# Forty-four unread one-pass products behind the low-rank gate product of layer one

## The chip, the cores and the metric

The kernel runs on one core of a Trainium2 chip. The metric is the device time of one execution in microseconds, as the median of several runs. A core has a matrix engine (TensorE; PE in the profile, and PEld for its loading of stationary operands), a vector engine (VectorE, DVE), an activation engine (ScalarE, ACT), a general engine (GpSimd, POOL) and a queue for transfers (SyncE, SP). Each works through its own list of instructions in order, and semaphores tie the lists together.

## The reference

The reference is two layers of an encoder trunk on 256 tokens and 16 learned meta tokens, D = 2048. Cut to what matters here:

```
def _layer(h, w_in, gla_w_up, gla_b_up, ...):
    proj = jnp.einsum('bld,dp->blp', h, w_in)
    gq, gk, gv, gr, glr, nq, nk, nv = jnp.split(proj, points, axis=-1)
    y_gla = _gla_mixer(gq, gk, gv, gr, glr, gla_w_up, gla_b_up, gla_norm_w)
    y_na = _na_mixer(nq, nk, nv, na_rel_bias)
    mix = jnp.einsum('blm,md->bld', jnp.concatenate([y_gla, y_na], axis=-1), w_out)
    h = _layer_norm(DEEPNORM_ALPHA * h + mix, ln1_w, ln1_b)
    ff = ... square(relu(h @ w_ff1)) @ w_ff2
    return _layer_norm(DEEPNORM_ALPHA * h + ff, ln2_w, ln2_b)

def _gla_mixer(q, k, v, r, gate_lr, w_up, b_up, norm_w):
    lr = gate_lr.reshape(B, L, 2, GLA_RANK)
    g = jax.nn.log_sigmoid(jnp.einsum('blzr,zrk->blzk', lr, w_up) + b_up) / GLA_TAU
    ...
```

The part of interest is `glr`: 32 columns of the input projection (rank 16, forward and backward), from which the decay gates of the linear attention are made. Everything is float32.

## The kernel before

**Precision.** A float32 operand is split into a high part of type fp32r and a low remainder of the same type. A product of two operands is then three one-pass products, high by high, high by low and low by high, accumulated in one PSUM bank. Weights come from memory in tiles of 128 x 1024 float32 (`raw`); ScalarE casts the high part (`wh`, line 217) and VectorE subtracts it to get the low part (`wl`, line 218). There are three buffers of each, and a tile is made while others are used. A tile holds eight blocks of 128 x 128 and feeds 24 products. The activations `x` lie in 16 pairs of high and low, 128 rows by 272 columns each (L = 272 tokens with the meta tokens).

**Narrow work.** Products with fewer than 256 columns (the intra-chunk scores, the neighbourhood attention, per-token sums) take plain float32 operands, with no split. Transposes go through TensorE against an identity matrix.

**The order.** The program is written out in one order. `by_k` computes four or eight outputs at once, over the 16 blocks of the contraction (line 303); `by_m` computes one output after another (`eight`, line 252; `sixteen`, lines 259 to 267). Between the pieces `pump` takes steps of two queues of generators, foreground and background, so that small work is strewn between the big products. In layer one `by_k` computes keys and the first half of the values, then `by_m` the second half of the values and the queries, while the foreground queue holds the generator `gates`.

**The gates.** `gates` has these steps: load the small weights; split the low-rank weights `wlr` into `ws`, 64 columns with 32 high and 32 low; then the low-rank product, 32 instructions at line 468, two for each of 16 blocks of x, into columns 0 to 271 of a bank `ps` of the four background banks. The output has 64 rows, high weights in the first 32 and low weights in the next. Then ScalarE copies rows 32 to 63 (`lrt`, line 473), VectorE adds the two halves (474), and `stack` makes `lr`, a high copy, a low copy and another high copy under one another (344, 345). In the next steps two products for each head (line 486) take `lr` and the up-projection, and ScalarE and VectorE make the gates from the result (487 to 492). In the same stretch `v_rows` transposes finished values (line 516).

The bank has 512 columns. Columns 272 to 511 of `ps` are not used.

Of the kernel before, what the change touches and what calls it, by code (L numbers as in the profile page):

```python
# [14 lines left out]
P = 128  # L15
D = 2048
DC = D // P
T = 256
NM = 16
L = T + NM  # L20
# [38 lines left out]
class Trunk:  # L59
# [392 lines left out]
    def gates(self):  # L452
        nc, e, l = self.nc, self.ep, self.l
        if l == 0:
            self.load_gates()
            self.consts()
        yield
        ws = e.tile([P, DC, 64], F32R, name="ws", tag="ws")
        self.split(self.wlr.rearrange("p (k c) -> p k c", c=32), ws[:, :, :32], ws[:, :, 32:])
        yield True  # L460
        uh = e.tile([LRK, 2, GH * GDK], F32R, name="uph", tag="uph")
        up = e.tile([LRK, 2, GH * GDK], F32R, name="up", tag="up")
        ps = self.bank()
        o = ps[:, :L]
        for k in range(DC):
            xh, xl = self.x[k]
            for m, r in ((64, xh), (32, xl))[::-1 if k == DC - 1 else 1]:
                nc.tensor.matmul(o[:m], lhsT=ws[:, k, :m], rhs=r[:, :L], start=k == 0 and m == 64,  # L468
                                 stop=k == DC - 1 and m == 64)
        t = e.tile([32, L], F32, name="lrt", tag="lrt")  # L470
        lr = e.tile([LRK, L], F32R, name="lr", tag="lr")
        nc.gpsimd.memset(lr[96:LRK, :].bitcast(F32), 1.0)
        nc.scalar.copy(t, o[32:64])
        nc.vector.tensor_tensor(t, o[:32], t, ALU.add)
        self.stack(t, lr, 32, (0, 64), 32)
        for d, w in enumerate(self.wup):
            w = w[:LRK]
            nc.scalar.copy(uh[:, d], w)
            nc.vector.tensor_scalar(w, w, self.sel[:, 0:1], None, ALU.mult)
            nc.vector.scalar_tensor_tensor(up[:, d], uh[:, d].bitcast(F32), self.sel[:, 1:2], w, ALU.mult, ALU.add)  # L480
        yield True
        for h in range(GH):
            z = [self.bank()[:, :L] for _ in range(2)]
            g = e.tile([P, 2, L], F32, name="gt", tag="gt", bufs=2)
            for d in range(2):
                nc.tensor.matmul(z[d], lhsT=up[:, d, h * GDK:h * GDK + GDK], rhs=lr, start=True, stop=True)
                nc.scalar.activation(g[:, d], z[d], AF.Abs)
            nc.scalar.activation(g, g, AF.Exp, scale=-1.0)
            nc.scalar.activation(g, g, AF.Ln, bias=self.one)
            for d in range(2):  # L490
                nc.vector.scalar_tensor_tensor(g[:, d], z[d], 0.0, g[:, d], ALU.min, ALU.subtract)
            nc.scalar.activation(self.decay[h], g, AF.Exp, scale=1 / TAU)
            yield h < GH - 1

    def ev_q(self, m, ps):
        self.nc.scalar.mul(self.qk[m][:, 1, :self.n], ps, GDK ** -0.5)
# [757 lines left out]
```

## Time and profile before

| | before |
|---|---|
| median of 3 runs | 2328.91 us |
| lowest and highest | 2328.5 and 2329.83 us |
| the profiled execution | 2329.64 us |
| span of its instructions | 2327.8 us |
| mean granted TensorE clock | 0.999 |
| busy: PE, PEld, DVE, ACT, POOL | 2318.9, 2202.1, 1522.8, 1222.8, 129.4 us |
| instructions on PE | 18052 |
| bytes moved | 419.01 MB |

The profile is one execution, with times from the start of its first instruction. A line such as "L252 PE MATMUL mm<-x,wh 128*128 128x272 f32" names the line of the kernel, the engine, the operation, the tiles written and read, the weights in rows by columns, and the moving operand in partitions by columns. Both plain float32 and fp32r stand as f32 in PE's rows; a plain float32 product has two records, a one-pass product has one. "Busy" is the time in which at least one instruction of the engine is in flight, and PE's instructions overlap, so the length of one is more than the step from one to the next.

### The profile page before, as it was taken

What the parts mean: (1) busy time and instruction counts of PE and PEld (TensorE: products, weight loads), DVE (VectorE), ACT (ScalarE), POOL (GpSimd) and SP (SyncE); (2) the same over time, 40 slices, a digit from 0 to 9 for tenths busy, and PEclk for the clock granted to TensorE, in tenths of its full rate; (3) what the DMA queues carried; (4) which work ended last, traced back from release to release, by engine and by line L of the source; (5) the groups of instructions that cost most, each with busy time, mean ns of one, the idle gap of its engine ahead of it and who ended that gap; (6) DMA issues with size and microseconds to landing.
All of it is one profiled execution on the core that took longest, in us unless ns stands there. A gap on an engine that the chain in (4) does not pass through costs nothing.

```text
span 2327.8 us, 44399 instructions
## 1 busy us (share of the span) xinstructions
PE 2318.9 (100%) x18052; PEld 2202.1 (95%) x18052; DVE 1522.8 (65%) x2440; ACT 1222.8 (53%) x2104; POOL 129.4 (6%) x200
## 2 busy tenths in 40 slices
PE   9999999999999999999999999999999999999998
PEld 9999999999999999999999899989988888888888
DVE  5588777775544455547576787778866545666655
ACT  5666665564433344444456666655655334555443
POOL 0021110110000000000020111100100000000000
PEclk9999999999999999999999999999999999999999
DMA  8554545555555566655555555555666565656664
GB/s 265 155 163 155 151 146 169 173 181 181 181 178 179 179 180 182 181 179 176 181 187 165 173 168 156 158 166 186 192 198 191 190 198 190 192 198 213 199 194 150
DMA packets 118300, 419.01 MB, mean 180 GB/s; under 512 B 13512, under 2 KB 14024, under 8 KB 118096
## 3 DMA queue, kind: packets, MB, share of 16 engines
q1 hardware_dynamic: 117808, 415.65, 57.2%
q8 instruction: 141, 2.31, 0.4%
q14 instruction: 63, 0.52, 0.1%
q10 hardware_dynamic: 288, 0.52, 0.1%
HBM read 414.03 MB, written 2.10 MB: 179 GB/s over the span
## 4 chain that ended last, share of the span: by engine, by line
PE 97%; DVE 1%; issue 1%; ACT 0%; DMA 0%; POOL 0%; DVEq 0%; ACTq 0%; SPq 0%; POOLq 0%
PE mm L252 56%; PE mm L264 30%; PE mm L303 4%; PE mm L313 2%; PE bg L303 1%; PE bg L827 1%; PE mm L766 1%; DVE wl L218 0%; PE bg L627 0%; PE bg L468 0%; DVE acc L1057 0%; PE mm L792 0%; PE bg L955 0%; PE mm L516 0%; PE bg L678 0%
## 5 line engine op out<-in xcount | busy, mean ns | idle before, releaser
L218 DVE TENSOR_TENSOR wl<-raw,wh 128x1024 fp32r<-128x1024 f32 (+1 forms) x770 | 938.3, 1225 | 645.1 <-ACT wh L217 546.0
L217 ACT CAST wh<-raw 128x1024 fp32r<-128x1024 f32 (+1 forms) x770 | 805.5, 1047 | 790.5 <-PE mm L252 383.8
L252 PE MATMUL mm<-x,wh 128*128 128x272 f32 (+3 forms) x4544 | 805.7, 294 | 0.0
L252 PEld LDWEIGHTS mm<-x,wh 128*128 128x128 f32 x4544 | 646.8, 188 | 14.9 <-PE mm L766 0.6
L252 PE MATMUL mm<-x,wl 128*128 128x272 f32 (+3 forms) x2432 | 519.7, 284 | 0.0
L252 PEld LDWEIGHTS mm<-x,wl 128*128 128x128 f32 x2432 | 390.8, 188 | 0.0
L252 PE MATMUL mm<-y,wh 128*128 128x272 f32 (+1 forms) x1440 | 235.0, 285 | 0.0
L252 PEld LDWEIGHTS mm<-y,wh 128*128 128x128 f32 x1440 | 199.7, 188 | 0.1
L264 PE MATMUL mm<-x,wh 128*128 128x512 f32 x832 | 193.8, 390 | 0.0
L264 PEld LDWEIGHTS mm<-x,wh 128*128 128x128 f32 x832 | 154.3, 188 | 31.0
L252 PE MATMUL mm<-u,wh 128*128 128x272 f32 (+1 forms) x1056 | 172.1, 285 | 0.0
L264 PE MATMUL mm<-y,wh 128*128 128x512 f32 x688 | 162.3, 389 | 0.0
L264 PEld LDWEIGHTS mm<-y,wh 128*128 128x128 f32 x688 | 128.6, 188 | 26.8 <-issue 0.4
L252 PE MATMUL mm<-y,wl 128*128 128x272 f32 (+1 forms) x720 | 146.5, 285 | 0.0
L252 PEld LDWEIGHTS mm<-u,wh 128*128 128x128 f32 x1056 | 146.3, 188 | 0.0
L264 PE MATMUL mm<-u,wh 128*128 128x512 f32 x496 | 118.3, 391 | 0.0
L252 PEld LDWEIGHTS mm<-y,wl 128*128 128x128 f32 x720 | 112.6, 188 | 0.0
L264 PEld LDWEIGHTS mm<-u,wh 128*128 128x128 f32 x496 | 90.9, 188 | 17.7
L252 PE MATMUL mm<-u,wl 128*128 128x272 f32 (+1 forms) x528 | 107.3, 284 | 0.0
L264 PEld LDWEIGHTS mm<-x,wl 128*128 128x128 f32 x832 | 98.4, 188 | 2.0
L264 PE MATMUL mm<-x,wl 128*128 128x256 f32 x832 | 98.8, 276 | 0.0
L264 PEld LDWEIGHTS mm<-y,wl 128*128 128x128 f32 x688 | 84.3, 188 | 3.0 <-DVE wl L218 0.2
(286 smaller groups left out, 2297.4 us busy)
## 6 DMA issues: line engine op xcount, KB each, us to landing
raw<-in_wff SPq DMA_DIRECT2D x512, 512.0 KB, 3.6
raw<-in_win SPq DMA_DIRECT2D x190, 512.0 KB, 4.0
raw<-in_wout SPq DMA_DIRECT2D x64, 512.0 KB, 3.6
nb<-in_nab SPq DMA_DIRECT2D x16, 352.0 KB, 4.3
xraw<-in_xT SPq DMA_DIRECT2D x7, 272.0 KB, 4.5
out<-out SPq DMA_DIRECT2D x5, 256.0 KB, 3.1
brow<-in_norm SPq DMA_DIRECT2D x4, 256.0 KB, 5.1
gw<-in_wup SPq DMA_DIRECT2D x4, 196.0 KB
```

What stands on the lines that cost most here:

```text
L217: self.nc.scalar.copy(h, r)
L218: self.wl = self.nc.vector.tensor_tensor(lo, r, h.bitcast(F32), ALU.subtract).ins
L252: mm(o, lhsT=self.block(w, j), rhs=rhs, start=first and not i, stop=last and i == len(TURNS[once]) - 1)
L264: self.nc.tensor.matmul(o, lhsT=self.block(both[j // 8][low], j % 8), rhs=rhs, start=first and not i + j, stop=bool(last and i and j == 15 ...
L303: self.nc.tensor.matmul(ps[g + m][:, :n], lhsT=self.block(parts[p][0], 4 * j + m if first else 2 * m + j), rhs=acts[k + j][parts[p][1]][:, ...
L313: self.nc.tensor.matmul(o, lhsT=self.block(both[low], i), rhs=rhs, start=not low and k + i % 2 == 0, stop=k == DC - 2 and i % 2 == 1 and n ...
L766: nc.tensor.matmul(ps[hh][:, t * NKEY:t * NKEY + NKEY], lhsT=q[hs, NM + t * P:NM + t * P + P], rhs=k[hs, t, :], start=True, stop=True)
L827: nc.tensor.matmul(po[t][hs, :P], lhsT=v2[ts, hs] if rest else v1[:, t, hs], rhs=p2[ts, hh, :] if rest else p1[:, 2 * hh + t, :], start=re ...
```

## The change

After the 32 instructions of the low-rank product of layer one, and before the copy that reads its result, 44 more products are issued. Number i takes as weights the first 128 columns of x block i modulo 16 and as moving operand the first n columns of the next block, the high parts for even i and the low parts for odd i. Each starts afresh and writes columns 272 to 271 + n of the same bank `ps`. Nothing reads these columns. The widths n are 128 twelve times, 136 twelve times, 240 and 128 in turn six times, and 64 eight times. The operands are of type fp32r. In layer two nothing is added.

```
@@ -467,6 +467,8 @@
             for m, r in ((64, xh), (32, xl))[::-1 if k == DC - 1 else 1]:
                 nc.tensor.matmul(o[:m], lhsT=ws[:, k, :m], rhs=r[:, :L], start=k == 0 and m == 64,
                                  stop=k == DC - 1 and m == 64)
+        if not l:
+            self.narrow(ps)
         t = e.tile([32, L], F32, name="lrt", tag="lrt")
         lr = e.tile([LRK, L], F32R, name="lr", tag="lr")
@@ -491,6 +493,13 @@
+
+    def narrow(self, ps):
+
+        sizes = [P] * 12 + [P + 8] * 12 + [240, P] * 6 + [64] * 8
+        for i, n in enumerate(sizes):
+            w, v = (self.x[(i + d) % DC][i % 2] for d in (0, 1))
+            self.nc.tensor.matmul(ps[:, L:L + n], lhsT=w[:, :P], rhs=v[:, :n], start=True, stop=True)
```

## The prediction

> **What bounds the kernel now.** I read the page first, then the busy time by stretches, the timeline around the place of the change, the chain of waits, and last the rows that can price a product the kernel does not contain yet.
>
> From the page: busy time by engine, two rows of the 40 slices, and the shares of the chain that ended last.
>
> ```profile
> span 2327.8 us, 44399 instructions
> ...
> PE 2318.9 (100%) x18052; PEld 2202.1 (95%) x18052; DVE 1522.8 (65%) x2440; ACT 1222.8 (53%) x2104; POOL 129.4 (6%) x200
> ...
> PE   9999999999999999999999999999999999999998
> ...
> PEclk9999999999999999999999999999999999999999
> ...
> PE 97%; DVE 1%; issue 1%; ACT 0%; DMA 0%; POOL 0%; DVEq 0%; ACTq 0%; SPq 0%; POOLq 0%
> ```
>
> TensorE is busy in 2318.9 of 2327.8 us, in every slice, at the full granted clock, and 97% of the chain is its matmuls. Busy is not the same as being at its pace, so I look at the stretches behind the change.
>
> ```profile
> 58.00:330.00 272.00, 272.00 (x2800) 267.31 (x2799) 207.75 (x444) 178.95 (x425) 38.90 (x67) 1.00 0.50 154
> 330.00:1197.00 867.00, 866.98 (x7097) 865.44 (x7096) 509.29 (x717) 397.73 (x587) 19.07 (x21) 1.00 0.58 179
> 1197.00:1220.00 23.00, 22.47 (x178) 22.25 (x177) 21.68 (x38) 17.27 (x33) 12.75 (x6) 1.00 0.44 150
> ```
>
> The columns after the stretch and its length are busy us of PE, PEld, DVE, ACT and POOL, then the clock, the share of the DMA engines and GB/s. From 58 us, where the low-rank product of layer one starts, up to 1197 us, PE is idle for 0.02 us in all. VectorE and ScalarE are free for a quarter to a half of the time, and the DMA engines about half. The first place where another engine sets the pace is the second normalisation of layer one, from 1197 us. So there are some 1,130 us behind the change in which nothing that TensorE does extra can fall into a gap.
>
> Now the place itself, from the timeline (start, length of the merged piece, engine, line), with all engines in it:
>
> ```profile
> 58.22 0.41 PE L252 MATMUL mm<-x,wl 128*128 128x272 f32 x2
> 58.34 3.99 PEld L468 LDWEIGHTS bg<-x,ws 128*64 128x64 f32 x32
> 58.42 1.05 ACT L217 CAST wh<-raw 128x1024 fp32r<-128x1024 f32 x1 [1.88 <-PE mm L252]
> 58.46 4.15 PE L468 MATMUL bg<-x,ws 128*64 128x272 f32 x32
> 59.50 1.23 DVE L218 TENSOR_TENSOR wl<-raw,wh 128x1024 fp32r<-128x1024 f32 x1 [1.39 <-ACT wh L217]
> 62.32 0.66 PEld L516 LDWEIGHTS mm<-ident,ft 128*128 128x128 f32 x6
> 62.45 0.82 PE L516 MATMUL mm<-ident,ft 128*128 128x128 f32 x6
> 62.65 0.38 ACT L473 COPY lrt<-bg 32x272 f32<-32x272 f32 x1 [3.18 <-PE bg L468]
> ...
> 63.03 0.75 PE L252 MATMUL mm<-x,wh 128*128 128x272 f32 x4
> ...
> 64.40 0.43 DVE L345 TENSOR_TENSOR lr<-lrt,lr 32x272 fp32r<-32x272 f32 x1
> ...
> 65.98 0.31 PEld L486 LDWEIGHTS bg<-lr,up 98*128 98x128 f32 x2
> ...
> 66.63 1.05 ACT L217 CAST wh<-raw 128x1024 fp32r<-128x1024 f32 x1
> ```
>
> PE goes from the 32 products of L468 without a break into six transposes and the next tile of weights. ScalarE has already stood 3.18 us in front of the copy at L473 that reads the result. The new products go into the joint at 62.3 us.
>
> **The change part by part.** *What it adds.* Only TensorE gets instructions: 44 products, each with its own load of 128 weight columns, once (the test is on layer one; the same place in layer two gets none). The moving columns are 12 times 128, 12 times 136, 6 times 240, 6 times 128 and 8 times 64: 5888 in all. No DMA, no tile, nothing on another engine. The operands are pieces of x, all 16 of which were read by the product just ahead, so there is no new wait for data. They write columns 272 up of a bank whose first 272 hold the low-rank result.
>
> *What one costs.* No row of the profile shows a one-pass (fp32r) product under 256 columns, so the price is bounded by neighbours:
>
> ```profile
> 1604.75 3.80 PE L264 MATMUL mm<-y,wl 128*128 128x256 f32 x32
> 1608.38 3.81 PE L264 MATMUL mm<-y,wh 128*128 128x512 f32 x16
> ```
>
> ```profile
> 1500.50 0.28 PE L252 MATMUL mm<-x,wl 128*128 128x256 f32 x1
> 1500.62 0.39 PE L252 MATMUL mm<-x,wh 128*128 128x512 f32 x1
> ```
>
> ```profile
> 2315.86 0.52 PEld L1128 LDWEIGHTS bg<-ones,s 128*128 128x128 f32 x4 [0.23 <-DVE s L982]
> ```
>
> ```profile
> 133.09 0.52 PEld L678 LDWEIGHTS bg<-S 128*128 128x128 f32 x4
> ```
>
> ```profile
> L468 PEld LDWEIGHTS bg<-x,ws 128*64 128x64 f32 x32 | 4.3, 135 | 0.5
> ...
> L678 PEld LDWEIGHTS bg<-S 128*128 128x128 f32 x32 | 4.2, 190 | 0.7
> ...
> L468 PEld LDWEIGHTS bg<-x,ws 128*32 128x32 f32 x32 | 3.5, 108 | 0.0
> ...
> L1128 PEld LDWEIGHTS bg<-ones,s 128*128 128x128 f32 x8 | 1.1, 190 | 0.3 <-DVE s L982 0.2
> ```
>
> The first row is the nearest of one pass: 32 products of 256 columns in a run. A merged piece of the timeline lasts from the first start to the last end; a single such product lasts 0.28 us (third row), so the step is (3.80 - 0.28) / 31 = 0.114 us, or 0.444 ns a column. A narrower one-pass product streams less, so as long as it is one pass it costs at most 0.114 us.
>
> The second row tells what happens when there is next to nothing to stream. L1128 multiplies 128 weight columns by a single column, and its four loads still take 0.52 us; one lasts 190 ns, so the step is (0.52 - 0.19) / 3 = 0.110 us. L678, with 128 columns, has the same 0.52 us for four. It is therefore the load that paces them. The lengths of loads say the same: 135 ns for 64 weight columns and 108 ns for 32 differ by 0.84 ns a column, which for 128 columns is 0.108 us of loading proper, the rest being a fixed lead that overlaps.
>
> A narrow product with 128 weight columns thus takes the larger of its load, 0.110 us, and its stream, at most 240 x 0.444 = 0.107 us. All 44 cost the same whatever their width: between 44 x 0.110 = 4.84 and 44 x 0.114 = 5.0 us. I take 0.112 us, because the widest of them stream as long as they load: 44 x 0.112 = **4.9 us**. Below zero is excluded: PE runs its instructions in order and has no idle time there to fill.
>
> [...]
>
> *What it moves.* The copy at L473 may now wait for the last narrow product instead of the last of L468, if the dependence is kept for the whole bank. Then ScalarE stands 3.18 + 4.9 = 8.1 us. Behind that copy on its queue are the eviction of a value tile and the weight cast that now starts at 66.63. Nobody misses it: PE uses no weights during the narrow products, and there are three weight buffers, the last of them being filled by the cast at 58.42 and the subtraction that ends at 60.73. The matmuls from 63.03 find three tiles ready, some 9 us of work (a tile is 24 products, about 3 us in the chain below), whenever they start. The chain from L473 to the ready lr takes from 62.65 to 64.83, and L486, which needs it, comes at 65.98: 1.15 us to spare, and if the copy waits, both ends shift together. If it does not wait, the chain gets 4.9 us more room. Either way it costs nothing. If that cover were gone, the price would be the late part of one cast and one subtraction, at most 1.05 + 1.23 = 2.3 us, once.
>
> ```profile
> 58.62 3.99 PE bg L468 x32
> 62.62 0.66 PE mm L516 x6
> 63.27 2.99 PE mm L252 x24
> 66.27 0.25 PE bg L486 x2
> 66.52 2.99 PE mm L252 x24
> ```
>
> The chain of waits shows that PE alone carries the path here. So the sum is the 4.9 us. The profiled execution took 2329.64 us (its span 2327.8 and 1.8 around it) and would take 2334.5. It lies 0.7 above the median of 2328.91 (2328.5 to 2329.83); on the median the forecast is 2328.91 + 4.9 = **2333.8 us**.
>
> **The rivals.** *More than one pass (2334.6 to 2340.2 us).* The kernel uses one-pass products only from 256 columns up and plain fp32 for everything narrower, so the trace cannot exclude that a narrow product falls back to several passes. Plain fp32 shows what that is: the 16 products that L678 has in the code are 32 records, each 0.11 us behind the last at 128 columns, which is 2 x 128 x 0.444. So it is four passes in two halves. Four passes here: the 5376 columns in products of 128 and more at 4 x 0.444 ns, 9.5 us, and 8 products of 64 at two loads each, 1.8 us: 11.3 us in all. Two passes in one record: 5376 x 0.888 ns = 4.8, and 8 x 0.112 = 0.9: 5.7 us. For it: no row below 256 columns. Against it: the 512-column row gives (3.81 - 0.39) / 15 = 0.228 us, twice the 0.114 of 256 columns (0.39 us is the length of a single one, in the row behind the 0.28), so that down to 256 nothing shows a change of mode.
>
> *Not slower: cost by columns (2331.5 us).* If loads can follow one another faster than 0.110 us for this kind of operand, because they are pulled ahead behind the products in flight, the narrow ones cost only their stream: 5888 x 0.444 ns = 2.6 us, or 0.11%. It decides as soon as the step of the load falls under 0.106 us (44 x 0.106 = 4.66 us). For it: loads do run ahead of the products, and PEld's records overlap. Against it: with one column, where nothing else is left, they still stand at 0.110. [...]
>
> *The clock falls (2338.8 us).* At the start PE runs at half pace:
>
> ```profile
> 1.21 3.54 PE L442 MATMUL bg<-zero 128*128 128x272 f32 x14 [1.21 <-DVE zero L439]
> ```
>
> ```profile
> L442 PE MATMUL bg<-zero x14: 428/428/596, 1.2 to 4.3; 128*128 128x272 f32 x14
> ```
>
> 14 products of 272 columns in 3.54 us, with 0.428 for the last (the line's median), are 0.239 us a step, against 0.114 x 272 / 256 = 0.121. If 5 us of load-bound products, which stream for only half of the time, counted as idleness, each would take about twice 0.112: 9.9 us in all. Against it: the row of the clock shows full speed through all the stages with transposes and narrow fp32 products.
>
> *Hidden or faster (2328.9 us or less).* The pause gives VectorE and ScalarE 4.9 us to catch up. It could be a gain only if PE waited for them soon after, and up to 1197 us it waits for 0.02 us.
>
> **How the numbers follow.** A measurement of this kernel tells about 0.2%, 4.66 us, from no change; the forecast of 4.9 lies just above. The pace of the load has 0.66: 0.55 slower, and 0.11 within the bound, when scatter of half a microsecond between runs takes it under 4.66. Several passes 0.19, the clock 0.03, both slower. Cost by columns 0.07, the same. Hidden 0.05, of which 0.02 the same and 0.03 faster. That makes faster 0.03, same 0.20, slower 0.77. The range goes from 2332.8 (44 x 0.110 = 4.84, less half a microsecond of scatter and the same again for the joint at either end) to 2340.2 (four passes). It leaves out cost by columns and hidden, 0.12, and a small tail of the first case.
>
> **What would show it.** The new line should have 44 matmuls and 44 loads between L468 and L516, the loads about 0.11 us apart throughout, in the 64-column products as in those of 240, 4.9 us from the first to the last; 88 records would mean two halves, steps of 0.03 to 0.1 us that follow the width would mean cost by columns. The transposes of L516 should start 4.9 us later than 62.45, the wait at L473 be 3.2 or 8.1 us, with PE's rows behind it unchanged but for the shift. I am wrong if the step follows the width, if the granted clock drops in that slice, or if a gap of PE appears at the next tiles of weights.

## The result and the profile after

| | before | after |
|---|---|---|
| median of 14 runs | 2329.79 us | 2334.19 us |
| lowest and highest | 2328.5 and 2330.49 | 2333.09 and 2335.97 |
| ratio after to before, 95% interval | | 1.0020, 1.0012 to 1.0028 |
| the profiled execution, its span | 2329.64, 2327.8 us | 2333.66, 2331.7 us |

The kernel became slower by 4.4 us (by the 95% interval 2.8 to 6.5). The forecast was 4.9 us on a base of 2328.91, which with more runs is 2329.79. Whether it is over or under the bound of 0.2% (4.66 us) the runs of this pair leave open: 4.4 lies under it, the interval reaches to both sides, and the 4.87 us read in the trace below lies over it.

The page of the kernel after, span and busy time by engine: PE has 44 instructions and 3.9 us more, its loads 3.7 us more, and the other engines are within 0.8 us of where they were.

```profile
span 2331.7 us, 44487 instructions
...
PE 2322.8 (100%) x18096; PEld 2205.8 (95%) x18096; DVE 1522.0 (65%) x2440; ACT 1222.3 (52%) x2104; POOL 129.5 (6%) x200
```

The timeline at the place of the change (after):

```profile
57.91 4.14 PE L468 MATMUL bg<-x,ws 128*64 128x272 f32 x32
...
61.77 5.00 PEld L502 LDWEIGHTS bg<-x,x 128*128 128x128 f32 x44
61.89 5.00 PE L502 MATMUL bg<-x,x 128*128 128x128 f32 x44
66.72 0.59 PEld L525 LDWEIGHTS mm<-ident,ft 128*128 128x128 f32 x6
66.72 0.87 PE L525 MATMUL mm<-ident,ft 128*128 128x128 f32 x6
66.92 0.38 ACT L475 COPY lrt<-bg 32x272 f32<-32x272 f32 x1 [8.01 <-PE bg L502]
...
67.35 0.75 PE L252 MATMUL mm<-x,wh 128*128 128x272 f32 x4
```

44 loads in 5.00 us, the last of them 0.19 us long, are (5.00 - 0.19) / 43 = 0.112 us a step, that is, from the start of one to the start of the next. From the start of L468 to the next weight tile it was 63.03 - 58.46 = 4.57 us before and is 67.35 - 57.91 = 9.44 now: **4.87 us** for the change at its own place. ScalarE stands 8.01 us in front of the copy, until the last narrow product is done, instead of 3.18. Over the change the granted clock (third figure from the end) is 1.00, and PE is busy without a gap up to 330 us:

```profile
61.80:66.70 4.90, 4.90 (x47) 4.90 (x44) 0.00 (x0) 0.00 (x0) 0.00 (x0) 1.00 0.27 99
57.00:330.00 273.00, 273.00 (x2813) 268.31 (x2812) 204.29 (x432) 176.06 (x415) 39.04 (x68) 1.00 0.50 153
```

Three pieces of the load queue of the same kernel, cut out of the groups of 136 columns, of 240 and 128 in turn, and of 64:

```profile
63.34 1.08 PEld L502 LDWEIGHTS bg<-x,x 128*128 128x128 f32 x9
```

```profile
64.68 1.08 PEld L502 LDWEIGHTS bg<-x,x 128*128 128x128 f32 x9
```

```profile
65.91 0.86 PEld L502 LDWEIGHTS bg<-x,x 128*128 128x128 f32 x7
```

(1.08 - 0.19) / 8 = 0.111, again 0.111, and (0.86 - 0.19) / 6 = 0.112 us. The width of the product does not appear in its price.

The chain of waits after, at the change, at the low-rank product of layer two, and at the start of the last stage:

```profile
58.07 3.98 PE bg L468 x32
62.05 4.83 PE bg L502 x44
...
1255.47 3.98 PE bg L468 x32
```

```profile
2318.76 0.98 PE mm L1124 x9
```

And the chain before, at the two places that were not shown:

```profile
1251.30 3.98 PE bg L468 x32
```

```profile
2314.89 0.98 PE mm L1115 x9
```

The profiled execution of the kernel after reached L468 0.55 us earlier than that of before (58.07 against 58.62), with the same program up to there. It lost 4.87 us at the change, is 4.17 us behind at layer two and 3.87 at the end. The 0.55 at the start and the 0.45 spread over 2250 us behind it lie within what executions differ by (the runs of before alone span 2.0 us); between layer two and the last stage it is 0.30, and no single place gives back what the change cost.

### The profile page after: what moved, and what is told of

It reads as the page before. It is cut to its first block, busy times and chain, and to the rows that moved or that the text cites. A ratio compares the mean times of both kernels' runs of the same rounds, so it can differ in the third digit from the quotient of the medians.

```text
span 2331.7 us, 44487 instructions
## 1 busy us (share of the span) xinstructions
PE 2322.8 (100%) x18096; PEld 2205.8 (95%) x18096; DVE 1522.0 (65%) x2440; ACT 1222.3 (52%) x2104; POOL 129.5 (6%) x200
## 4 chain that ended last, share of the span: by engine, by line
PE 97%; DVE 1%; issue 1%; ACT 0%; DMA 0%; POOL 0%; SPq 0%; DVEq 0%; ACTq 0%; POOLq 0%
PE mm L252 56%; PE mm L264 30%; PE mm L303 4%; PE mm L313 2%; PE bg L303 1%; PE bg L836 1%; PE mm L775 1%; DVE wl L218 0%; PE bg L636 0%; DMA raw<-in_win 0%; PE bg L468 0%; DVE acc L1066 0%; PE mm L801 0%; PE bg L964 0%; PE mm L525 0%
```

## The experiments

All kernels keep the place of the change and alter only what is issued there, or the bank it is written to; nobody reads those products. In the code, (...) marks what is left out. "Above" is a median, or a single run where said, against the runs of the kernel before on the same chip. Those runs spread by up to 2.9 us, so where there is a single run the trace decides and not the total. "Stream" is the time in which the moving columns pass through the array, an estimate at the 0.444 ns a column that the products of 256 columns in the prediction gave.

**1. All 64 columns wide.**

```
-        sizes = [P] * 12 + [P + 8] * 12 + [240, P] * 6 + [64] * 8
+        sizes = [64] * 44
```

> The 44 products stay, each with 128 weight columns, but all have 64 moving columns (2816 columns in place of 5888). Theory, the pace of the weight load: the step stays 0.112 us and the whole is again 4.9 us above the kernel before. Rival, cost by columns: 2816 x 0.444 ns = 1.25 us, steps of 0.03 us.

Measured: 2336.27 us, 6.7 above, ratio 1.0029 (1.0018 to 1.0041). Neither expectation names that. But the seven runs fall apart: three at 2334.14 to 2335.05, median 4.9 above, with a mean granted clock of 0.999 or 1.000, and four at 2336.27 to 2338.01, all with 0.998. The one profiled in detail, at 2336.27, has the same 44 loads:

```profile
61.99 5.00 PEld L502 LDWEIGHTS bg<-x,x 128*128 128x128 f32 x44
```

5.00 us for less than half of the columns: cost by columns is excluded. What is new lies behind them. Stretches of this run; the granted clock stands before the last two figures:

```profile
64.00:67.00 3.00, 3.00 (x29) 3.00 (x28) 0.00 (x0) 0.00 (x0) 0.00 (x0) 1.00 0.00 0
67.00:68.00 1.00, 1.00 (x7) 0.85 (x7) 0.43 (x1) 0.38 (x1) 0.00 (x0) 0.55 0.00 0
68.00:69.00 1.00, 1.00 (x6) 1.00 (x5) 0.04 (x1) 0.73 (x3) 0.00 (x0) 0.50 0.00 0
69.00:70.00 1.00, 1.00 (x6) 1.00 (x5) 0.82 (x2) 0.94 (x4) 0.00 (x0) 0.50 0.00 0
70.00:71.00 1.00, 1.00 (x8) 1.00 (x8) 0.64 (x2) 0.59 (x2) 0.00 (x0) 0.75 0.00 0
```

From 67.1 to 70.5 us TensorE runs at half clock (0.55 over the first of these microseconds and 0.75 over the last give the two ends). It is the rival "the clock falls", in a kernel that differs from the change only in width. Experiments 9 to 11 follow it.

**2. Half of the weight columns.**

```
-            self.nc.tensor.matmul(ps[:, L:L + n], lhsT=w[:, :P], rhs=v[:, :n], start=True, stop=True)
+            self.nc.tensor.matmul(ps[:64, L:L + n], lhsT=w[:, :64], rhs=v[:, :n], start=True, stop=True)
```

> Widths as in the change, but each product loads 64 weight columns in place of 128 and writes 64 rows. Theory, the pace of the load: a load step of 0.056 us, so each product costs the larger of that and 0.444 ns a moving column: 12 x 0.057 + 12 x 0.060 + 6 x 0.107 + 6 x 0.057 + 8 x 0.056 = 2.8 us above the kernel before. Rival, a fixed cost of about 0.11 us for any product whatever its load: 4.9 us.

Measured: 2333.11 us, 3.6 above, ratio 1.0015 (1.0006 to 1.0023). The runs alone can't part 2.8 from 4.9 (the interval is 1.4 to 5.4 us above); the chain can:

```profile
62.04 2.96 PE bg L502 x44
```

2.96 us where it was 4.83. The weight columns carry the price, and a fixed cost of 0.11 us for each product is excluded.

**3. Plain fp32.**

```
+            (... lhsT=w[:, :P].bitcast(F32), rhs=v[:, :n].bitcast(F32) ...)
```

> The same 44 products on plain fp32 operands. Four passes in two records each: 88 loads and 88 matmuls, 5376 columns x 4 x 0.444 ns + 8 x 2 x 0.112 us = 11.3 us above the kernel before. Rival, that the load paces these too and the passes are hidden: 88 x 0.112 = 9.9 us, with the 240-column ones no longer than the others.

Measured: 2340.29 us, 10.7 above, ratio 1.0047 (1.0035 to 1.0060). The chain has 88 products in 10.96 us:

```profile
62.24 10.96 PE bg L502 x88
```

That is near the four passes (11.3) and over the load alone (9.9). So the rival "more than one pass" was priced well, and the change is not it: 44 records in 4.83 us.

**4. Four times as many.**

```
-        sizes = [P] * 12 + [P + 8] * 12 + [240, P] * 6 + [64] * 8
+        sizes = 4 * ([P] * 12 + [P + 8] * 12 + [240, P] * 6 + [64] * 8)
```

> The list of 44 products is issued four times, 176 in all. Theory: 176 x 0.112 = 19.7 us above the kernel before, all of it on the path, and the granted clock stays at 1.0. Rival, cost by columns: 10.5 us. Rival, the clock: 20 us of products that stream for half of the time let it fall, steps of 0.22 us appear after some microseconds, and the whole is 25 to 39 us. Rival, part of a long pause is given back later: under 18 us.

Measured: 2349.17 us, 19.6 above, ratio 1.0085 (1.0071 to 1.0099):

```profile
63.65 19.57 PE bg L502 x176
```

The local price and the total agree, 4.9 us for each 44, and the mean granted clock stayed at 0.999 to 1.000. By the interval (16.5 to 23.1 us) a return of some 3 us isn't excluded, but nothing points to one.

**5. A sweep of widths.**

```
+        own = self.bank()
+        sizes = [n for n in (16, 32, 64, 128, 192, 224, 240, 248, 256, 264, 272) for _ in range(8)]
+            (... own[:, :n], lhsT=w[:, :P], rhs=v[:, :n] ...)
```

> The list is replaced by 88 products in a bank of their own, eight each of 16, 32, 64, 128, 192, 224, 240, 248, 256, 264 and 272 moving columns, each with 128 weight columns. Theory, the larger of load and stream: a step of 0.112 us from 16 up to about 248 columns and from there 0.444 ns a column: 0.114 at 256, 0.117 at 264, 0.121 at 272; with no jump at 256. About 10 us in all. Rival, a change of mode under 256 columns: a jump between 248 and 256.

Measured: 2339.27 us, one run, 9.5 above. Six loads out of the groups of 16, 240, 248, 256 and 272 columns, in this order:

```profile
61.82 0.75 PEld L503 LDWEIGHTS bg<-x,x 128*128 128x128 f32 x6
```

```profile
67.18 0.75 PEld L503 LDWEIGHTS bg<-x,x 128*128 128x128 f32 x6
```

```profile
68.07 0.77 PEld L503 LDWEIGHTS bg<-x,x 128*128 128x128 f32 x6
```

```profile
69.00 0.78 PEld L503 LDWEIGHTS bg<-x,x 128*128 128x128 f32 x6
```

```profile
70.92 0.81 PEld L503 LDWEIGHTS bg<-x,x 128*128 128x128 f32 x6
```

(0.75 - 0.19) / 5 = 0.112 us at 16 and at 240, then 0.116 at 248, 0.118 at 256 and 0.124 at 272: flat, and then rising with the width, with no jump between 248 and 256. The rising part starts a little earlier than expected; at 256 and 272 columns it is 0.003 to 0.004 us above the rule of 0.444 ns a column.

**6. A sweep of weight columns.**

```
+        own = self.bank()
+        sizes = [c for c in (32, 64, 96, 128) for _ in range(11)]
+            (... own[:n, :P], lhsT=w[:, :n], rhs=v[:, :P] ...)
```

> The list is replaced by 44 products of 128 moving columns in a bank of their own, eleven each with 32, 64, 96 and 128 weight columns. Theory, the larger of the stream (128 x 0.444 ns = 0.057 us) and the load (0.87 ns a weight column): steps of 0.057, 0.057, 0.084 and 0.112 us. Rival, a fixed cost for any product: 0.11 us in all four groups.

Measured: 2331.97 us, one run, 2.2 above. Nine loads out of each group:

```profile
61.75 0.59 PEld L503 LDWEIGHTS bg<-x,x 128*32 128x32 f32 x9
```

```profile
62.41 0.61 PEld L503 LDWEIGHTS bg<-x,x 128*64 128x64 f32 x9
```

```profile
63.09 0.84 PEld L503 LDWEIGHTS bg<-x,x 128*96 128x96 f32 x9
```

```profile
64.05 1.09 PEld L503 LDWEIGHTS bg<-x,x 128*128 128x128 f32 x9
```

With 0.107, 0.135, 0.165 (an estimate, midway between its neighbours) and 0.19 us for a single load the steps are 0.060, 0.059, 0.084 and 0.112 us. Up to 64 weight columns the step doesn't follow the load; it is near the stream of 128 columns (0.057). From 96 on it follows the load.

**7. The same bytes as bf16.**

```
+            (... lhsT=w.bitcast(mybir.dt.bfloat16)[:, :P], rhs=v.bitcast(mybir.dt.bfloat16)[:, :n] ...)
```

> The same 44 products and widths, but the operands are read as 2-byte bf16 values (the first half of the same bytes, so other numbers, which nothing reads). If the step of the load hangs on 4-byte weights, it falls well under 0.112 us: a step of 0.057 us for 128 columns by the stream alone, 2.6 us in all. [...] If the load is paced by columns alone, 4.9 us.

Measured: 2331.93 us, one run, 2.1 above.

```profile
62.57 2.62 PEld L502 LDWEIGHTS <-x 128*128 128x128 bf16 x44
```

44 loads in 2.62 us: the stream alone (5888 x 0.444 ns = 2.6). The seven last loads, all of the group of 64 columns, show how far the price falls:

```profile
64.91 0.27 PEld L502 LDWEIGHTS <-x 128*128 128x128 bf16 x7
```

(0.27 - 0.098) / 6 = 0.029 us for 128 weight columns and 64 moving ones, where it was 0.112. In these runs the flat price belongs to the 4-byte weights. It isn't the bytes alone: 64 columns of 4 bytes, as many bytes, would by the proportion of experiment 6 have a load step of an estimated 0.056 us, half of 0.112. The load itself is shorter, 98 ns in the median in place of 192; why it is so is not shown. On average a product takes 2.62 / 44 = 0.060 us with bf16 and 0.112 with fp32r.

**8. A bank of their own.**

```
+        own = self.bank()
-            self.nc.tensor.matmul(ps[:, L:L + n], ...
+            self.nc.tensor.matmul(own[:, L:L + n], ...
```

> The 44 products write a bank of their own, so the copy of the low-rank result need not wait for them. Theory: the wait in front of that copy goes back from 8.0 to 3.2 us, and the time stays 4.9 us above the kernel before, since the copy's wait costs nothing. Rival, the longer wait of ScalarE costs or gives something further on: a change of some tenths to 2 us against the change.

Measured: 2334.38 us, 4.6 above, ratio 1.0019 (1.0010 to 1.0029), against 4.4 for the change.

```profile
62.97 0.38 ACT L475 COPY lrt<-bg 32x272 f32<-32x272 f32 x1 [3.18 <-PE bg L468]
...
68.46 0.39 ACT L513 COPY ft<-mm 128x272 f32<-128x272 f32 x1 [3.75 <-PE mm L526]
```

The wait is back at 3.18 us, and the time differs by no more than the runs can tell (their interval is 2.3 to 6.8 us above). ScalarE merely waits at a later instruction for the same PE.

**9 to 11. Three times as many, of 64, 96 and 128 columns.**

```
+        sizes = [64] * 132      (and 96, and 128)
```

> 132 products of 64 columns with 128 weight columns. In the run with 44 of them the granted clock fell for one window of 3.4 us just behind them in some executions (2336.27 to 2338.01 us) and not in others (2334.14 to 2335.05). Theory, the clock follows the share of the time in which the array streams, here 0.028 of 0.112 us, 25%: 14.7 us contain whole windows in every execution, the clock falls within 3.4 to 6.8 us and stays down, loads then stand 0.224 us apart, and with 72 to 102 products at that pace the whole is 22 to 29 us above the kernel before, in every execution. Rival, the drop has another cause and the clock stays: 14.7 us.

> 132 products of 96 columns: the array streams 0.043 of 0.112 us, 38%. Either the clock holds and it is 132 x 0.112 = 14.7 us above the kernel before, or it falls as with 64 columns, 22 to 29 us. Theory gives no side: this and the next run say where between 25% and 100% the point lies.

> 132 products of 128 columns: the array streams 0.057 of 0.112 us, 51%. The four-fold list, with 8 products of 64 columns at a time among wider ones, kept the clock, so it holds here too: 132 x 0.112 = 14.7 us above the kernel before, loads 0.112 us apart from the first to the last. Rival: at half the time it falls, 22 to 29 us.

Measured: 2355.69, 2353.99 and 2345.14 us, 26.2, 24.5 and 15.6 above, ratios 1.0112 (1.0092 to 1.0131), 1.0104 (1.0084 to 1.0124) and 1.0064 (1.0045 to 1.0084). Two stretches of each, of 64, 96 and 128 columns:

```profile
64.40:67.80 3.40, 3.40 (x31) 3.40 (x30) 0.00 (x0) 0.00 (x0) 0.00 (x0) 0.94 0.01 4
67.80:71.20 3.40, 3.40 (x18) 3.40 (x17) 0.00 (x0) 0.00 (x0) 0.00 (x0) 0.50 0.00 0
```

```profile
64.40:67.80 3.40, 3.40 (x33) 3.40 (x33) 0.00 (x0) 0.00 (x0) 0.00 (x0) 1.00 0.00 0
67.80:71.20 3.40, 3.40 (x20) 3.40 (x20) 0.00 (x0) 0.00 (x0) 0.00 (x0) 0.57 0.00 0
```

```profile
64.40:67.80 3.40, 3.40 (x33) 3.40 (x32) 0.00 (x0) 0.00 (x0) 0.00 (x0) 1.00 0.05 22
67.80:71.20 3.40, 3.40 (x33) 3.40 (x32) 0.00 (x0) 0.00 (x0) 0.00 (x0) 1.00 0.00 0
```

With 64 and with 96 columns the clock falls to half some 5 to 6 us into the stretch, and the instructions in 3.4 us go from 31 or 33 to 18 or 20; with 128 it holds to the end. PE is busy for all 3.40 us in all three. The kernels differ in the width alone, and with it in the share of the time in which the array streams. At 0.444 ns a column and 112 ns a step that is an estimated 25%, 38% (96 x 0.444 / 112) and 51%.

**12. One set of weights for all.**

```
-            w, v = (self.x[(i + d) % DC][i % 2] for d in (0, 1))
+            w, v = self.x[0][0], self.x[(i + 1) % DC][i % 2]
```

> The 44 products of the change, all with the same 128 weight columns (those of x block 0). Theory: each product loads its weights again, 44 loads 0.112 us apart, 4.9 us above the kernel before. Rival, a load of what is already there is skipped or short: 2.6 us, the stream alone.

Measured: 2333.46 us, one run, 3.9 above; in the chain as long as in the change:

```profile
61.90 4.84 PE bg L502 x44
```

Weights that are there already are loaded again and cost the same, 4.84 us where it was 4.83.

## Why the prediction was right, point by point

*What bounds the kernel.* Right: the whole price of the products shows in the total, most exactly with four times as many, 19.57 us in the chain and 19.6 between the medians.

*What one costs.* Right, and shown rather than argued: 0.112 us whatever the width from 16 to 240 columns, proportional to the weight columns from 96 to 128 (0.084 and 0.112 us), near the stream below that (0.060 and 0.059 against an estimated 0.057) and with 2-byte weights (44 loads in 2.62 us against an estimated 2.6). The one-column products at the end of the kernel before were the row to read. The measured 4.4 us for the change against 4.87 in its trace fits scatter: the kernel with a bank of its own has 4.6, the three runs of the first experiment that kept the clock 4.9, and a quarter of the fourth 4.9; the single run with one set of weights has 3.9. That the forecast of 2333.8 us came within 0.4 of the measured 2334.19 is partly luck, since the base was 0.9 too low and the price 0.5 above what the runs show. The rule of 0.444 ns a column is a little low above the flat part, and a row shown in the prediction told it: 24 products of 272 columns in 2.99 us are 0.125 us each and not 0.121. For the widths of the change that makes no difference.

*What it moves.* Right. The copy did wait, 8.01 us of the 8.1 forecast, and taking that wait away changed nothing that the runs can tell.

*More than one pass.* Did not happen. Two passes in one record would set products of 240 columns 240 x 0.888 ns = 0.213 us apart, and they stand 0.112 apart. The four-pass price stood up with plain operands, 10.96 us in the chain against 11.3.

*Cost by columns.* Excluded by the first experiment: 2816 columns take the same 5.00 us of loads as 5888.

*The clock falls.* Did not happen in the profiled execution of the change, nor by the mean clock (0.999 or 1.000) in any of its 14 runs. But the reason given against it did not carry. The prediction pointed to full speed through all stages with transposes and narrow fp32 products. In those stages wide products stand between the narrow ones: from 296.51 to 299.92 us of the kernel before, among narrow fp32 work, 16 products of 272 columns stream for an estimated 16 x 272 x 0.444 ns = 1.9 of 3.4 us. So they did not test what a run of narrow products alone does. The half pace at the start of the kernel, which the rival set out from, stands in the trace at a granted clock of 1.00 (1.20 to 4.70 us), though its loads last 331 ns in the median, as at half clock in experiments 9 and 10 (333); what slowed it is not shown, and that idleness did was an assumption. The change streams for 5888 x 0.444 ns = 2.6 of its 4.9 us, an estimated 53%, while in experiments 10 and 11 an estimated 38% lost the clock and 51% kept it. With all 44 products at 64 columns four executions of seven came out 1.8 to 3.6 us above the median of the others. The chance of 0.03 was too small for a stretch that stood so near the edge, and the price of 9.9 us too high for 5 us: in the profiled run of the first experiment the clock fell only as the products ended, and what it slowed was the work behind.

## What to carry to other kernels

A one-pass product with 4-byte operands and 128 weight columns had a floor in these runs, 0.112 us from 16 to 240 moving columns, under which narrowing the moving side bought nothing. Fewer weight columns did (0.059 us with 64 of them and 128 moving ones), and so did 2-byte operands (0.029 us with 64 moving ones). To price a kind of instruction that a trace lacks, look for a row in which its other cost has almost vanished, here one moving column. And before such products are strung together for some 5 us, the shortest stretch that lost its clock here, work out the share of the time in which the array streams: in experiments 9 and 10 PE was busy for 3.40 of 3.40 us at a granted clock of 0.50.

## What was not expected of the hardware

The granted clock fell to 0.50 while PE never idled, in both profiled runs of 132 products of 64 or 96 columns (loads then last 333 ns in the median in place of 192), and not with 128 columns; all six runs of the first two have a mean clock of 0.994 or 0.995, the three of the last 0.999 or 1.000. Behind 44 products of 64 columns the drop lasted about 3.4 us, from 67.1 to 70.5, and came in some executions and not in others. The stretches before, at and behind half clock, with 64 and with 96 columns:

```profile
64.00:67.41 3.41, 3.41 (x33) 3.41 (x33) 0.00 (x0) 0.00 (x0) 0.00 (x0) 1.00 0.04 18
67.41:91.30 23.89, 23.89 (x113) 23.74 (x113) 2.27 (x6) 3.14 (x10) 0.00 (x0) 0.50 0.00 1
91.30:94.71 3.41, 3.41 (x29) 3.41 (x29) 1.23 (x1) 2.69 (x5) 0.00 (x0) 1.00 0.00 0
```

```profile
64.84:68.25 3.41, 3.41 (x33) 3.41 (x33) 0.00 (x0) 0.00 (x0) 0.00 (x0) 1.00 0.00 0
68.25:88.73 20.48, 20.48 (x98) 20.33 (x98) 1.28 (x3) 2.07 (x7) 0.00 (x0) 0.50 0.00 1
88.73:92.14 3.41, 3.41 (x29) 3.41 (x29) 1.34 (x4) 2.51 (x7) 0.00 (x0) 1.00 0.00 0
```

Half clock lasted 3.4 us in the first experiment, and here 23.89 = 7 x 3.413 and 20.48 = 6 x 3.413 us: in these three profiles a whole number of stretches of one length, by estimate. The stretch of 3.41 us ahead of each fall lay wholly in narrow products. By the chain of waits these began at 62.28, 62.43 and 62.81 us, and the clock fell at 67.1, 67.41 and 68.25, which is 4.8, 5.0 and 5.4 us later, so not at a fixed time behind their start. Why 5.0 us of products lost the clock in four executions of seven and kept it in three is not shown. What the runs do show is that PE was not idle ahead of a fall (busy for 3.41 of 3.41 us): the clock fell with an estimated 25% and 38% of streaming and stayed up with 51%, with loads in flight for 3.40 of 3.40 us from 67.80 to 71.20 in experiments 9 to 11. Where between 38% and 51% the point lies, and whether loads count for a part, stays open.
